# A written order for the output projection and the passage to up, scaling a step behind the store, and transposes in 64-row pairs, in a hybrid decoder block

## The chip, the cores and the metric

The kernel runs on one core of one Trainium2 chip. The metric is device time in microseconds (us) of one execution. The kernel before takes 2476.66 us, the median of three runs (2476.07 to 2476.84).

## The reference

One decoder layer on x (2048 rows of 1024, float32):

```python
mod = c_act @ w_ada[l] + b_ada[l]
sh1, sc1, gt1, sh2, sc2, gt2 = [m[:, None, :] for m in jnp.split(mod, 6, axis=-1)]
h = rms_norm(x, g_mix[l]) * (1.0 + sc1) + sh1
y = hybrid_mixer(h, w_in[l], ...)          # ends in y @ w_out
x = x + gt1 * y
h = rms_norm(x, g_ffn[l]) * (1.0 + sc2) + sh2
x = x + gt2 * conv_ffn(h, w_up[l], w_conv[l], b_conv[l], w_down[l])
```

The change concerns the stretch between the mixer and the feed-forward part: y @ w_out, the gated residual, the second RMSNorm with its scale and shift, and the turn of h into the layout (channels on partitions) that the up product reads.

## The kernel before, in words

All float32 products are made of three passes over values split in a high and a low part (`mm3`, L53): the matmuls on L54, L55 and L56, high times high, high times low, low times high. A split is a ScalarE copy into the high part and a VectorE subtraction into the low part.

The kernel has these stages in order of time: the first projection and the mLSTM and gating groups, the attention, the output projection (from about 1019 us), the passage to up, up with its convolution and gate, and down. From up on, products follow a scheme with seven products in place of eight, on sums and differences of quarters of h, called B11, B21, B22, T1, T2, T3 and T4.

The output projection works on four blocks of 512 rows, in the order `TBS = (2, 3, 0, 1)` (`n` is 0 to 3). A block is eight steps. A step is one row tile `i` (128 rows) times one half `nb` of the 1024 columns: 8 x 3 matmuls of 128x512 into one of four banks of PSUM (`Block.mm`, L1449, tiles wps). The order of (i, nb) is by halves in block 0 (all four tiles with nb = 0, then all with nb = 1), by tiles in blocks 1 and 2, and by pairs of tiles in block 3.

One step later the result is evicted on VectorE (`evict`, L1460). For nb = 0 it is multiplied with gt1 (L1465) and added to x (L1466); for nb = 1 the weights already hold gt1, and one addition does (L1468). ScalarE squares the half and sums it (L1469). After nb = 1 the row tile is stored to x2_d (L1471), `stats` (L1473) makes the RMS factor with two small VectorE operations and one power on GpSimd, and `scale` (L1479, L1481) multiplies the whole row tile with it, in place, so after its store has been read. Only the last two row tiles of block 3 are scaled into a fresh tile.

When the four row tiles of a block are scaled, `turns` (L1494) puts them through PE: per 128 columns `k`, `turn` (L1484) makes four 128x128 transposes into one bank (tile tps, four of them), and one ScalarE activation (L1490) applies scale and shift and writes the tile hz. Each block has two groups of four `turn`, put in behind its successor's second and third step. Block 3's eight `turn` stand in the passage, between up products.

For the second half of the rows (blocks 0 and 1) the parts of h are split and stored for later (`put`, L1421, `put_d`, L1436, to hc_d); `turns` puts them in the list `todo`, and `some` takes a few operations' worth of it at each step. The tiles that hold a split (tag w, four of them) later hold the first up weights (`w_load`, L344, called at step 3 of block 3).

Beside that, `load_w` (L314) loads the second half of w_out in eight parts, multiplies each with gt1 (L302) and splits it (L136, L137) into the sixteen tiles wo1; and `y_load` (L1317) and `y_split` (L1321) load, add and split the next block's eight y parts. Both use five load buffers (tag ld).

Each engine works through its own queue in order. SP issues all DMAs, also in order, and waits at an issue until the data or the buffer is free. Up to step 3 of block 3 a scheduler of the framework decides the order in which the recorded instructions stand on each engine. From step 4 of block 3 on they stand as the program writes them (`manual_schedule`, L1885), through the passage (L1923 to L2037) and until step 14 of up.

Of the kernel before, what the change touches and what calls it, by code (L numbers as in the profile page):

```python
# [8 lines left out]
F32 = mybir.dt.float32  # L9
F32R = mybir.dt.float32r  # L10
# [7 lines left out]
P = 128  # L18
# [15 lines left out]
def trunk(  # L34
# [254 lines left out]
    def load_parts(src, more=None):  # L289
        t = pool.tile([P, TB], F32, name="ld", tag="ld")  # L290
        dma(t, src)
        if more is None:
            return t, None
        t2 = pool.tile([P, TB], F32, name="ld", tag="ld")
        dma(t2, more)
        return t, t2

    def split_parts(t, t2, tag, eng, pair=False, gain=None):
        if t2 is not None:
            eng.tensor_tensor(t, t, t2, op=ALU.add)  # L300
        if gain is not None:
            eng.tensor_tensor(t, t, gain, op=ALU.mult)  # L302
# [11 lines left out]
    def load_w(nb, gain=None):  # L314
        for k in range(KT):
            src = w_out[k * P : (k + 1) * P, nb * 512 : nb * 512 + 512]
            eng = V if gain is not None else (G, V)[k % 2]
            wo.append(split_parts(*load_parts(src), "wo%d" % nb, eng, gain=gain))
# [1002 lines left out]
    def y_split(n=9):  # L1321
        while loaded_y and n:
            n -= 1
            n, k, parts = loaded_y.pop(0)
            ys.setdefault(n, {})[k] = split_parts(*parts, "act%d" % ((4 if n % 2 else 14) + k), V, pair=True)

    order = (
        "SUSSXSUVSUSSXSUXVSSSXVVYUSXSSTVXSUSVSXSSUWVXWUWXVXSSXUVYUWUXWVUWVWXUSSXSXSVVXVSXZSSSVVUSSUXWXVSSSXSV"
        "VVYUSSXSXVVVWUYSSXUVVVXSSWUWVXSSXSVUUWTVUXSSXSXSVVVZSXSXUWXVSSUYWVVXUUWVSSSXSVVXUSXSUVVWSSXSVXVSSZSV"
# [91 lines left out]
    def put(n, q, t):  # L1421

        if n == "T2":
            src = t[:, 1, :].bitcast(F32)
            V.tensor_tensor(src, h_part("B22", q), h_part("T1", q), op=ALU.subtract)
            V.tensor_tensor(h_part("T4", q), h_part("B21", q), src, op=ALU.subtract)
        else:
            src = h_part(n, q)
            if n == "T1":
# [3 lines left out]
        A.copy(t[:, 0, :], src)  # L1433
        V.tensor_tensor(t[:, 1, :], src, t[:, 0, :].bitcast(F32), op=ALU.subtract)

    def put_d(n, q):  # L1436
        t = pool.tile([P, 2, 512], F32R, name="hl", tag="w")
        put(n, q, t)
        dma(hc_d[COMBO.index(n), q], t.bitcast(F32))

    class Block:
        def __init__(self, n, tb):
# [3 lines left out]
        def rows(self, i):  # L1446
            return slice(self.tb * TB + i * P, self.tb * TB + i * P + P)

        def mm(self, i, nb):  # L1449
            if i not in self.x:  # L1450
                self.x[i] = pool.tile([P, D], F32, name="x2")
                dma(self.x[i], x[self.rows(i), :])
                self.st[i] = pool.tile([P, 2], F32, name="st", tag="wst_")
            sl = slice(i * P, (i + 1) * P)
# [26 lines left out]
            V.tensor_scalar(t, self.x[i], self.st[i][:, 0:1], None, op0=ALU.mult)  # L1481
            self.xn[i] = t

        def turn(self, k):  # L1484
            if self.half == 0:
                hT[k] = pool.tile([P, 1024], F32, name="hz", tag="zy")
            ps = pp.tile([P, 512], F32, name="tps", tag="tps")
            for i in range(4):
                T.transpose(ps[:, i * P : (i + 1) * P], self.xn[i][:, k * P : (k + 1) * P], ident)
            A.activation(  # L1490
                hT[k][:, self.half * 512 : self.half * 512 + 512], ps, AF.Identity, bias=sh2[:, k : k + 1], scale=a2[:, k : k + 1]
            )

        def turns(self, ks):  # L1494
            for k in ks:
                self.turn(k)
            names = ("T1", "T3", "T2", "T4", "B22") if self.half else ("B11", "B21")
            for group in (("T1",), ("B11",)) if ks[0] == 0 else (("T3",), ("T2", "T4", "B22"), ("B21",)):
                for q in range(4):
                    for n in group:  # L1500
                        if self.H == 1 and n in names:
                            ops = {"T1": 2, "T3": 2, "T2": 3}.get(n, 1)
                            todo.append((ops, lambda n=n, q=q: put_d(n, q)))

    hb = {}

# [18 lines left out]
            b_low(n, q)  # L1525

    def some(ops):
        while todo and ops > 0:
            n, f = todo.pop(0)
            ops -= n  # L1530
            f()

    def up_open_left():
        pool.open(
# [5 lines left out]
    class Group:  # L1540
# [37 lines left out]
        def prep(self, p):  # L1578
            self.sums(p)
            self.high(p)  # L1580
            self.low(p)
# [297 lines left out]
    prev = before = None  # L1879
    written = ExitStack()  # L1880
    for n, tb in enumerate(TBS):
        blk = Block(n, tb)
        for j, (i, nb) in enumerate((by_nb, by_i, by_i, by_two)[n]):
            if (n, j) == (3, 4):
                written.enter_context(tc.manual_schedule())  # L1885
            blk.mm(i, nb)
            if (n, j) == (0, 0):
                load_w(1, gt1[:, 512:1024])
            if (n, j) == (3, 3):
                w_first = [w_load(0), w_load(1)]  # L1890
            if prev:
                prev[0].evict(*prev[1:])
            y_split()
            if prev and prev[2] == 1:
                prev[0].stats(prev[1])
            some({1: 2, 2: 5, 3: 3}.get(n, 0))
            if (n, j) == (3, 7):
                prep(4)
            if prev and prev[2] == 1:
                prev[0].scale(prev[1], pool.tile([P, D], F32, name="x2") if (n, j) == (3, 7) else None)  # L1900
            if (n, j) == (3, 5):
                pool.close("wo_r")
                up_open_right()
                for _ in range(AHEAD):
                    up_groups(-1)
            if (n, j) == (3, 6):
                for m in range(4):
                    prep(m)
            if before and j in ((2, 3) if n == 3 else (1, 2)):
                assert n < 3 or not todo  # L1910
                before.turns(range(4) if j == (2 if n == 3 else 1) else range(4, 8))
            if n == 3 and j in (4, 5):
                b_first(("B11", "B21")[j - 4])
            if n < 3:
                for k in ({3: (0, 1), 4: (2, 3), 5: (4, 5), 6: (6, 7)}.get(j, ()) if n == 0 else {5: (5, 6), 6: (7,), 7: ()}.get(j, (j,))):
                    y_load(n + 1, k)
            prev = (blk, i, nb)
        before = blk
    assert not todo and not loaded_y
    blk.evict(3, 1)  # L1920
    blk.stats(3)
# [14 lines left out]
    at(7, "high")  # L1936
    blk.turn(0)
    b_diff("T1", 0)
    blk.turn(1)
    b_high("T1", 0)  # L1940
    b_diff("T1", 1)
    at(7, "low")
    for q in (2, 3):
        blk.turn(q)
        b_high("T1", q - 1)
        b_low("T1", q - 2)
        b_diff("T1", q)
# [1 line left out]
    blk.turn(4)  # L1949
    b_high("T1", 3)  # L1950
    b_low("T1", 2)
    blk.turn(5)
    b_low("T1", 3)
    b_diff("T2", 0)
    blk.turn(6)
    blk.turn(7)
    pp.close("wo_l")
    pp.open("up_l", "left", ("ub1", 2048, 4))
    pool.close("wo_l")
# [154 lines left out]
```

## Time and profile before

| | |
|---|---|
| median of three runs | 2476.66 us |
| the profiled execution, its time | 2478.34 us |
| the profiled execution, its span | 2476.6 us |
| PE busy | 2443.3 us, 99% |
| VectorE busy | 1876.7 us, 76% |
| ScalarE busy | 1198.8 us, 48% |
| granted PE clock, mean | 0.998 |
| output projection | 1019 to 1211 us of the span |
| passage to up | 1211 to 1250 us of the span |

The span is from the first to the last instruction of the profiled execution; the rest of its time lies around it. An engine's busy time counts its instructions' run times; PE's matmuls overlap each other, so that a busy PE is not a PE at its peak. A row of the time-line has start, length, engine, line, operation, tiles written and read, shape, and in brackets the idle time before it and who ended it. In the names, wps is a bank of the projection, tps one of the transposes, x a row tile, hz a turned tile, ub a bank of up.

### The profile page before, as it was taken

Reading aid. Unit: us, or ns where it says so; the run is one execution under the profiler, and the core shown is the slowest. Engines: PE = TensorE matmul, PEld = TensorE weight load, DVE = VectorE, ACT = ScalarE, POOL = GpSimd, SP = SyncE. Lnnn points to the kernel's source line nnn. Section 1 sums busy time; section 2 is a strip of 40 time slices with the busy share of each in tenths; the row PEclk is TensorE's granted clock in tenths of the full one; section 3 lists DMA queues with packets and bytes.
Section 4 is the critical chain, followed back from the end, with each engine's and each line's share of the span. In section 5 each row is a group of like instructions: output and inputs, shape, how many; then the busy total and the mean of one; then the engine's idle time right before and its main releaser. Section 6 shows DMA issues by size and latency. Waiting matters only on the chain.

```text
span 2476.6 us, 38891 instructions
## 1 busy us (share of the span) xinstructions
PE 2443.3 (99%) x14297; PEld 1984.7 (80%) x14297; DVE 1876.7 (76%) x3170; ACT 1198.8 (48%) x2068; POOL 379.7 (15%) x417
## 2 busy tenths in 40 slices
PE   6999999999999999999999999999999999999999
PEld 6888888888766666788878888888888888888887
DVE  6657656476377777756799888879888878988897
ACT  5443343433267778544554544445444445444443
POOL 2023310133257665200000000000000000000000
PEclk9999999999999999999999999999999999999999
DMA  8345753545665453677332222282222229387523
GB/s 271 105 148 164 219 170 91 152 139 162 160 171 152 118 164 107 209 252 285 100 103 86 85 85 77 85 314 94 77 85 85 86 95 319 126 285 238 174 73 119
DMA packets 297271, 373.48 MB, mean 151 GB/s; under 512 B 31358, under 2 KB 190044, under 8 KB 296056
## 3 DMA queue, kind: packets, MB, share of 16 engines
q1 hardware_dynamic: 297080, 371.00, 47.6%
q8 instruction: 112, 1.84, 0.3%
q14 instruction: 79, 0.65, 0.1%
HBM read 274.34 MB, written 96.58 MB: 150 GB/s over the span
## 4 chain that ended last, share of the span: by engine, by line
PE 86%; DVE 6%; DMA 5%; ACT 2%; issue 1%; POOL 0%; SPq 0%; DVEq 0%; ACTq 0%; POOLq 0%
PE ub L55 11%; PE ub L56 11%; PE ub L54 11%; PE acc L54 6%; PE acc L56 6%; PE acc L55 6%; PE db L55 5%; PE db L56 5%; PE db L54 5%; PE op L266 5%; PE pr L218 5%; PE pr L248 3%; DMA x_d<-x 1%; PE wps L56 1%; PE wps L54 1%
## 5 line engine op out<-in xcount | busy, mean ns | idle before, releaser
L54 PE MATMUL acc<-wh,hh 128*128 128x512 f32 (+2 forms) x752 | 279.2, 372 | 0.0
L54 PE MATMUL ub<-T,wsph 128*128 128x512 f32 x704 | 273.8, 389 | 1.2 <-ACT wsph L1572 1.2
L55 PE MATMUL ub<-T,wsph 128*128 128x512 f32 x704 | 274.3, 390 | 0.2 <-DVE T L1520 0.2
L56 PE MATMUL ub<-T,wspl 128*128 128x512 f32 x704 | 273.9, 389 | 0.0
L56 PE MATMUL acc<-wh,hl 128*128 128x512 f32 (+2 forms) x752 | 270.0, 361 | 0.3 <-DVE hl L586 0.2
L55 PE MATMUL acc<-wl,hh 128*128 128x512 f32 (+2 forms) x752 | 268.7, 359 | 0.6 <-DVE wl L628 0.6
L55 PE MATMUL db<-wspl,wsph 128*128 128x512 f32 x616 | 239.9, 390 | 0.1
L56 PE MATMUL db<-wsph,wspl 128*128 128x512 f32 x616 | 239.6, 389 | 0.0
L54 PE MATMUL db<-wsph 128*128 128x512 f32 x616 | 239.5, 389 | 0.0
L1572 ACT CAST wsph<-S 128x512 fp32r<-128x512 f32 x176 | 109.6, 624 | 219.0 <-PE ub L55 153.8
L1715 ACT CAST wsph<-act 128x512 fp32r<-128x512 f32 x154 | 96.3, 626 | 228.6 <-PE db L55 218.7
L55 PE MATMUL ub<-B,wsph 128*128 128x512 f32 x528 | 205.6, 389 | 1.0 <-DVE B L1520 0.9
L54 PE MATMUL ub<-B,wsph 128*128 128x512 f32 x528 | 205.7, 390 | 0.0
L56 PE MATMUL ub<-B,wspl 128*128 128x512 f32 x528 | 205.4, 389 | 0.0
L224 DVE CUSTOM_DVE_ANT_0 L<-pr,nf 128x1024 f32<-128x1024 f32 (+7 forms) x128 | 124.4, 989 | 67.7 <-PE pr L223 31.3
L232 ACT ACTIVATE L<-L,nm 128x1792 f32<-128x1792 f32 (+15 forms) x128 | 153.7, 1204 | 21.1 <-DVE nm L224 20.3
L56 PEld LDWEIGHTS acc<-wh,hl 128*128 128x128 f32 x752 | 142.3, 190 | 22.2 <-DVE hl L586 0.9
L55 PEld LDWEIGHTS acc<-wl,hh 128*128 128x128 f32 x752 | 142.8, 190 | 20.4 <-DVE wl L628 1.5
L54 PEld LDWEIGHTS acc<-wh,hh 128*128 128x128 f32 x752 | 142.8, 190 | 19.7 <-issue 0.7
L54 PEld LDWEIGHTS ub<-T,wsph 128*128 128x128 f32 x704 | 132.2, 188 | 29.2 <-ACT wsph L1572 1.6
L55 PEld LDWEIGHTS ub<-T,wsph 128*128 128x128 f32 x704 | 132.1, 188 | 28.7 <-DVE T L1520 1.5
L56 PEld LDWEIGHTS ub<-T,wspl 128*128 128x128 f32 x704 | 132.2, 188 | 27.5 <-DVE wspl L1576 0.3
(331 smaller groups left out, 5535.1 us busy)
## 6 DMA issues: line engine op xcount, KB each, us to landing
w<-in_w_up_dram SPq DMA_DIRECT2D x88, 512.0 KB
wd<-in_w_down_dram SPq DMA_DIRECT2D x154, 256.0 KB
wa<-in_w_ada_dram SPq DMA_DIRECT2D x96, 256.0 KB
act_d<-yc SPq DMA_DIRECT2D x44, 512.0 KB
act<-act_d SPq DMA_DIRECT2D x44, 512.0 KB
wr<-in_w_in_dram SPq DMA_DIRECT2D x64, 256.0 KB
q<-q_d SPq DMA_DIRECT2D x128, 128.0 KB
hc_d<-hl SPq DMA_DIRECT2D x28, 512.0 KB
```

What stands on the lines that cost most here:

```text
L54: T.matmul(ps, lh, rh, start=start, stop=False, skip_group_check=resume)
L55: T.matmul(ps, lh, rl, start=False, stop=False, skip_group_check=resume)
L56: T.matmul(ps, ll, rh, start=False, stop=stop, skip_group_check=resume)
L218: T.matmul(dst, q2[a][r, qs], kk[b][r, ks], start=n == 0, stop=n == 2 and not (last and f == own))
L224: V.tensor_tensor_reduce(out=L[:, c * 1024 : c * 1024 + w], in0=sp[:, o : o + w], in1=nf[:, c * 1024 + o : c * 1024 + o + w], scale=-1.0, ...
L232: A.activation(L, L, AF.Exp, bias=nm[:, n : n + 1], scale=-1.0, accum_out=rs)
L248: T.transpose(tp[:, f, to : to + 64], L_[h, tb, i][0][r, o : o + P], ident[r, r])
L266: T.matmul(op_[h, tb][r].rearrange("p (f n) -> p f n", f=2)[:, :, c0:], vv_[h // 2][:, 2 * p + j, h % 2 * 64 : h % 2 * 64 + 64], pT[:, :, ...
L1572: A.copy(self.wa[p][0], self.source(p))
L1715: A.copy(hi, v)
```

## The change

All of it lies between the end of the attention and the passage.

**Written order.** The whole output projection now stands as the program writes it. A step is, in this order: the low parts still held from the step before (`settle`); the matmuls; the scale of the row tile whose statistics were made a step before; the eviction of the step before; the splits of the step (`run`: y parts that have been loaded, in the first three steps of block 0 three parts of w1 each, and some of `todo`), where each task has a first VectorE operation, a ScalarE copy and a low part that is held until the next task's copy is issued; the loads of the next y parts; the load of the next x row tile (`want`); the statistics. Of `todo` four operations are taken per step in blocks 2 and 3 (before, five and three).

**Scaling.** `scale` follows one step behind `stats`, in place as before. In the last four steps of block 3 every row tile except the first is scaled into a fresh tile (before, the last two).

**Transposes.** `turn` takes two `k` at once. Each 128x128 transpose becomes two transposes of 64 rows, lower and upper half into two banks (tile tps, now two pairs of banks), as `turn_pair` (L238) does in the attention. The activation reads both banks.

```diff
+    def w1_task(k):
+        t = w1_parts[k]
...
+        return (
+            lambda: V.tensor_tensor(t, t, gt1[:, 512:1024], op=ALU.mult),
+            lambda: A.copy(hi, t),
+            lambda: V.tensor_tensor(lo, t, hi.bitcast(F32), op=ALU.subtract),
+        )
...
-    pp.open("wo_l", "left", ("tps", 2048, 4))
+    pp.open("wo_l", "left", ("tps", 4096, 2))
+    written = ExitStack()
+    written.enter_context(tc.manual_schedule())
+    for _ in range(5):
+        w1_load()
...
-        def turn(self, k):
...
-            for i in range(4):
-                T.transpose(ps[:, i * P : (i + 1) * P], self.xn[i][:, k * P : (k + 1) * P], ident)
...
+        def turn(self, k0):
+            ps = pp.tile([P, 2, 512], F32, name="tps", tag="tps")
+            for m in range(2):
+                k = k0 + m
...
+                for i in range(4):
+                    at = m * 256 + i * 64
+                    for f, r in enumerate((lower, upper)):
+                        T.transpose(ps[:, f, at : at + 64], self.xn[i][r, k * P : (k + 1) * P], ident[r, r])
+            for m in range(2):
+                k = k0 + m
+                to = hT[k][:, self.half * 512 : self.half * 512 + 512].rearrange("p (i f c) -> p f i c", f=2, c=64)
+                A.activation(
+                    to, ps[:, :, m * 256 : m * 256 + 256].rearrange("p f (i c) -> p f i c", c=64), AF.Identity,
+                    bias=sh2[:, k : k + 1], scale=a2[:, k : k + 1],
+                )
...
+    def run(tasks):
+        for first, high, low in tasks:
+            first()
+            high()
+            settle()
+            held.append(low)
+
+    def settle():
+        while held:
+            held.pop(0)()
...
+    for r, (n, j, i, nb) in enumerate(walk[:28]):
+        blk, before = blocks[n], blocks[n - 1] if n else None
+        settle()
+        blk.mm(i, nb)
+        if normed:
+            normed[0].scale(normed[1])
+            normed = None
+        tasks = [y_task() for _ in range(len(loaded_y))]
+        if prev:
+            prev[0].evict(*prev[1:])
+        if n == 0 and j < 3:
+            tasks += [w1_task(k) for k in range(3 * j, min(3 * j + 3, KT))]
+        tasks += some({1: 2, 2: 4, 3: 4}.get(n, 0))
+        run(tasks)
...
+        for k in y_wanted.get((n, j), ()):
+            y_load(n + 1, k)
+        n2, _, i2, _ = walk[r + 1]
+        if r < 27:
+            blocks[n2].want(i2)
+        if prev and prev[2] == 1:
+            prev[0].stats(prev[1])
+            normed = prev[:2]
...
+        if prev[2] == 1:
+            prev[0].scale(prev[1], pool.tile([P, D], F32, name="x2"))
```

How the rows move is shown at three places; outside the projection and the passage the order of PE, VectorE and ScalarE is the same in both programs, and VectorE's number of instructions too. First, PE at block 0's first group of transposes (x_13156 to x_13304 are its four row tiles, x_13168 to x_13309 in the change). Before:

```order
L54 MATMUL wps<-wo1h,yhl 128x512
L55 MATMUL wps<-wo1l,yhl 128x512
L56 MATMUL wps<-wo1h,yhl 128x512
L1489 MATMUL tps<-ident,x_13156 128x128
L1489 MATMUL tps<-ident,x_13240 128x128
L1489 MATMUL tps<-ident,x_13272 128x128
L1489 MATMUL tps<-ident,x_13304 128x128
```

After the change:

```order
L54 MATMUL wps<-wo1h,yhl 128x512
L55 MATMUL wps<-wo1l,yhl 128x512
L56 MATMUL wps<-wo1h,yhl 128x512
L1528 MATMUL tps<-ident,x_13168 128x64 x2
L1528 MATMUL tps<-ident,x_13216 128x64 x2
L1528 MATMUL tps<-ident,x_13263 128x64 x2
L1528 MATMUL tps<-ident,x_13309 128x64 x2
```

The group stands at the same place; it has 32 transposes of 64 rows (x2 is the pair of halves) for 16 of 128.

Second, VectorE at the end of block 0 (L1481 and L1516 are the scale, L1468 and L1503 the eviction of nb = 1, L300 and L1347 the sum of a y part, L137 and L1349 its low part). Before:

```order
L1475 TENSOR_TENSOR st<-st 128x1
L1476 TENSOR_SCALAR st<-st 128x1
L137 TENSOR_TENSOR yhl<-ld,yhl 128x512 x2
L1481 TENSOR_SCALAR x_13272<-x_13272,st 128x1024
L300 TENSOR_TENSOR ld<-ld 128x512
L1468 TENSOR_TENSOR x_13304<-wps,x_13304 128x512
L137 TENSOR_TENSOR yhl<-ld,yhl 128x512 x2
L1475 TENSOR_TENSOR st<-st 128x1
L1476 TENSOR_SCALAR st<-st 128x1
L137 TENSOR_TENSOR yhl<-ld,yhl 128x512 x3
L1481 TENSOR_SCALAR x_13304<-x_13304,st 128x1024
L1465 TENSOR_TENSOR yg<-wps,gt_13154 128x512
```

After the change:

```order
L1503 TENSOR_TENSOR x_13263<-wps,x_13263 128x512
L1510 TENSOR_TENSOR st<-st 128x1
L1511 TENSOR_SCALAR st<-st 128x1
L1349 TENSOR_TENSOR yhl<-ld,yhl 128x512
L1516 TENSOR_SCALAR x_13263<-x_13263,st 128x1024
L1503 TENSOR_TENSOR x_13309<-wps,x_13309 128x512
L1510 TENSOR_TENSOR st<-st 128x1
L1511 TENSOR_SCALAR st<-st 128x1
L1516 TENSOR_SCALAR x_13309<-x_13309,st 128x1024
L1500 TENSOR_TENSOR yg<-wps,gt_13166 128x512
```

The scale of row tile i stands ahead of the eviction of row tile i+1 in both; fewer y operations lie between.

Third, VectorE in block 3, around the scale of its second row tile (B is the split of a part of h). Before:

```order
L1468 TENSOR_TENSOR x_14364<-wps,x_14364 128x512
L1475 TENSOR_TENSOR st<-st 128x1
L1476 TENSOR_SCALAR st<-st 128x1
L1481 TENSOR_SCALAR x_14364<-x_14364,st 128x1024
L1468 TENSOR_TENSOR x_14408<-wps,x_14408 128x512
L1475 TENSOR_TENSOR st<-st 128x1
L1476 TENSOR_SCALAR st<-st 128x1
L1481 TENSOR_SCALAR x_14408<-x_14408,st 128x1024
L1520 TENSOR_TENSOR B_14604<-hz,B_14604 128x512
```

After the change:

```order
L1503 TENSOR_TENSOR x_14392<-wps,x_14392 128x512
L1510 TENSOR_TENSOR st<-st 128x1
L1511 TENSOR_SCALAR st<-st 128x1
L1516 TENSOR_SCALAR x_14392<-x_14392,st 128x1024
L1503 TENSOR_TENSOR x_14438<-wps,x_14438 128x512
L1510 TENSOR_TENSOR st<-st 128x1
L1511 TENSOR_SCALAR st<-st 128x1
L1516 TENSOR_SCALAR x_14687<-x_14438,st 128x1024
L1563 TENSOR_TENSOR B_14689<-hz,B_14689 128x512
```

The second row tile's scale now writes another tile (x_14687) than the one that is being stored (x_14438).

More of the change, by code (lines that the diff above doesn't have):

```diff
@@ L312, in trunk, with w1_load @@
     wo = []
[L314 to L318, printed above, removed]
+    w1_parts = []
+    def w1_load():
+        k = len(w1_parts)
+        if k < KT:
+            w1_parts.append(load_parts(w_out[k * P : (k + 1) * P, 512:1024])[0])
+    def w1_task(k):
+        t = w1_parts[k]
+        wo.append((pool.tile([P, TB], F32R, name="wo1h", tag="wo1"), pool.tile([P, TB], F32R, name="wo1l", tag="wo1")))
+        hi, lo = wo[8 + k]
+        return (
[3 more added lines that the diff above has]
+        )
     def up_open_right():
@@ L1432, in put, with low @@
                 V.tensor_tensor(src, h_part("B22", q), h_part("B12", q), op=ALU.subtract)
[L1433 to L1439, printed above, removed]
+        def low():
+            V.tensor_tensor(t[0][:, 1, :], source(), t[0][:, 0, :].bitcast(F32), op=ALU.subtract)
+            dma(hc_d[COMBO.index(n), q], t[0].bitcast(F32))
+        return first, lambda: A.copy(t[0][:, 0, :], source()), low
     class Block:
@@ L1527, in some @@
     def some(ops):
+        tasks = []
         while todo and ops > 0:
-            n, f = todo.pop(0)
+            n, q = todo.pop(0)
             ops -= n
-            f()
+            tasks.append(put_task(*q))
+        return tasks
+    held = []
+    def run(tasks):
[7 more added lines that the diff above has]
+            held.pop(0)()
     def up_open_left():
@@ L1878, in trunk @@
     by_two = [(i + m, nb) for m in (0, 2) for nb in range(2) for i in range(2)]
[L1879 to L1918, printed above, removed]
@@ new lines, in trunk @@
+    for j, (i, nb) in enumerate(by_two):
+        if j < 4:
+            continue
+        blk.mm(i, nb)
+        if normed:
+            normed[0].scale(normed[1])
+            normed = None
+        prev[0].evict(*prev[1:])
+        if prev[2] == 1:
+            prev[0].stats(prev[1])
+        if j == 7:
+            prep(4)
+        if prev[2] == 1:
+            prev[0].scale(prev[1], pool.tile([P, D], F32, name="x2"))
+        if j == 5:
+            pool.close("wo_r")
+            up_open_right()
+            for _ in range(AHEAD):
+                up_groups(-1)
+        if j == 6:
+            for m in range(4):
+                prep(m)
+        if j in (4, 5):
+            b_first(("B11", "B21")[j - 4])
+        prev = (blk, i, nb)
```

69 lines of the change are left out of this document (48 added, 21 removed).

## The prediction, on record before the change was run

> **What bounds the kernel now.** I read the page's first part, then the stretches around the change, then TensorE's (PE's) time-line there, then the chain of waits. In the page's first part and in a table of stretches, the columns are busy microseconds by engine (PE, weight loads, VectorE, ScalarE, GpSimd), granted clock, DMA share, GB/s.
>
> ```profile
> span 2476.6 us, 38891 instructions
> PE 2443.3 (99%) x14297; PEld 1984.7 (80%) x14297; DVE 1876.7 (76%) x3170; ACT 1198.8 (48%) x2068; POOL 379.7 (15%) x417
> ...
> 1019.00:1211.00 192.00, 190.68 (x890) 158.77 (x889) 117.71 (x210) 82.27 (x165) 10.34 (x16) 1.00 0.70 238
> 1211.00:1250.00 39.00, 37.33 (x176) 29.58 (x175) 37.14 (x61) 24.71 (x46) 0.17 (x1) 1.00 0.36 108
> 1250.00:1312.00 62.00, 62.00 (x274) 51.13 (x273) 61.33 (x81) 36.18 (x62) 0.00 (x0) 1.00 0.29 94
> ```
>
> PE is the bound, at full clock. The output projection runs from 1019 to 1211, and PE lacks only 1.3 us of 192 there; VectorE has 74 us to spare. In the passage to up (1211 to 1250) both are nearly full: VectorE 37.1 of 39, PE 37.3. So the projection gets shorter only by shorter PE work or by the 1.3 us, and the passage only by what VectorE lets through. Behind 1250 VectorE is as full as PE, so what arrives there as a shift stays a shift.
>
> Where PE's time goes besides the matmuls is in the eight groups of transposes. The rows: start, length, engine, line, tiles, count, idle before and its cause.
>
> ```profile
> 1073.60 0.49 PE L1489 MATMUL tps<-ident,x 128*128 128x128 f32 x3
> 1074.84 1.64 PE L1489 MATMUL tps<-ident,x 128*128 128x128 f32 x13 [0.75 <-DVE x L1481]
> 1076.23 0.48 PE L54 MATMUL wps<-wo0h,yhl 128*128 128x512 f32 x1
> 1076.55 0.39 PE L55 MATMUL wps<-wo0l,yhl 128*128 128x512 f32 x1
> 1076.78 0.40 PE L56 MATMUL wps<-wo0h,yhl 128*128 128x512 f32 x1
> ...
> 1081.81 1.91 PE L1489 MATMUL tps<-ident,x 128*128 128x128 f32 x16
> 1083.47 0.48 PE L54 MATMUL wps<-wo1h,yhl 128*128 128x512 f32 x1
> ...
> 1121.69 0.49 PE L1489 MATMUL tps<-ident,x 128*128 128x128 f32 x3
> 1122.75 1.64 PE L1489 MATMUL tps<-ident,x 128*128 128x128 f32 x13 [0.57 <-DVE x L1481]
> 1124.15 0.48 PE L54 MATMUL wps<-wo0h,yhl 128*128 128x512 f32 x1
> ```
>
> From the first transpose to the next matmul, an undisturbed group of 16 lasts 1083.47 - 1081.81 = 1.66 us, 104 ns each. The first group lasts 2.63 and the third 2.46: at the fourth transpose PE waits for the last scaled row tile (L1481). The second, fourth, fifth and sixth are undisturbed. Matmuls follow each other in 0.23 us (1076.55 to 1076.78), the first behind a group in 0.32. Six groups lie in the projection and cost 2.63 + 2.46 + 4 x 1.66 = 11.73 us; two lie in the passage.
>
> **Part 1, the transposes.** Each 128-row transpose becomes two of 64 rows. The kernel has this form already, in the attention (L248), same shapes, halves alternating:
>
> ```profile
> 1008.63 1.27 PE L248 MATMUL pr<-ident,L 64*128 64x64 f32 x34
> 1009.83 3.02 PE L266 MATMUL op<-pT,vv 128*64 128x512 f32 x16
> ...
> 1012.78 1.40 PE L248 MATMUL pr<-ident,L 64*128 64x64 f32 x38
> 1014.10 1.30 PE L266 MATMUL op<-pT,vv 128*64 128x512 f32 x8
> ```
>
> 34 take 1.20 us until the next matmul, 38 take 1.32: 30 ns for one more, and some 0.18 us fixed, with a change of array shape at each end. A group of 32 then takes 1.20 - 2 x 0.03 = 1.14 us instead of 1.66. Bounds: 0.96 (no fixed part) and 1.32 (the row of 38). Undisturbed, six groups cost 6.84 us: 11.73 - 6.84 = 4.89 us less, if the two waits go (Part 2). The bounds move this by +1.1 and -1.1. ScalarE still reads each group with four instructions of 512 columns; with 82 of 192 us busy it hides them behind the next step's 5.6 us of PE (1076.23 to 1081.81). If it did not, the second group of a block would wait for its bank pair.
>
> The Trainium skill, page "TensorEngine Tiling (Array Packing)", section "Key Properties", speaks against the change: switching the tiling mode drains the array, and here every group brings two switches that the 128-row form lacks. The fixed 0.18 us above contains two switches; by the rule alone a 128 x 128 neighbour could cost more, which is the third rival.
>
> **Part 2, scaling a step behind the store.** The row tile is stored unscaled and then scaled in place, so each scale waits for its store. VectorE in block 0, and the stores in the chain of waits:
>
> ```profile
> 1048.87 0.68 DVE L1468 TENSOR_TENSOR x<-wps,x 128x512 f32<-128x512 f32 x1
> 1054.65 0.75 DVE L1481 TENSOR_SCALAR x<-x,st 128x1024 f32<-128x1024 f32 x1
> 1055.32 0.68 DVE L1468 TENSOR_TENSOR x<-wps,x 128x512 f32<-128x512 f32 x1
> ...
> 1069.22 0.69 DVE L1468 TENSOR_TENSOR x<-wps,x 128x512 f32<-128x512 f32 x1
> 1074.03 0.75 DVE L1481 TENSOR_SCALAR x<-x,st 128x1024 f32<-128x1024 f32 x1 [0.18 <-DMA x_d<-x]
> ...
> 1049.69 4.86 DMA x_d<-x
> 1056.03 5.34 DMA x_d<-x
> 1062.84 5.01 DMA x_d<-x
> ...
> 1098.40 3.71 DMA x_d<-x
> 1118.23 3.62 DMA x_d<-x
> ```
>
> Eviction to store takes 0.82 (1048.87 to 1049.69), scale to next eviction 0.67. The scale of row i stands ahead of the eviction of row i+1, now and in the change (second piece of order above), so in block 0, which takes its second halves in a run, the four stores stay in series: last scale = first eviction + 4 x (0.82 + store) + 3 x 0.67 = first eviction + 5.3 + 4 stores. With 4.8 us a store this gives 1073.4; the trace has 1074.03.
>
> In the change, what differs is the start and the store. The start: from gt1's arrival VectorE has the same 30-odd operations in both.
>
> ```profile
> 1028.54 1.90 DVE L302 TENSOR_TENSOR ld<-ld,gt 128x512 f32<-128x512 f32 x3 [8.72 <-DMA gt<-gt_d]
> 1042.91 3.87 DMA ld<-y_d
> ```
>
> SP still issues the same five weight loads and then gt1, so VectorE still begins at 1028.5. In the written order each step's eviction stands first and low parts wait for their own ScalarE copy; the third y part needs the fifth-last load buffer and so stands behind one load (3.87). I put the first eviction 1.7 us later, 1050.6 (bounds 1048.9 and 1051.4). The store: now y loads are issued whenever one of five buffers falls free, beside the stores; in the change each y part is asked for one step ahead and its low half is held, so that fewer are under way. I take 4.0 us, near the lone stores (3.62 and 3.71; upper bound 5.34). The last scale ends at 1050.6 + 5.3 + 16 + 0.75 = 1072.7; PE wants it where its idle time began, at 1074.84 - 0.75 = 1074.1. Up to a store of 4.3 us the wait is gone, and the next thing late is nothing on VectorE but PE itself. The third group's wait goes with more room: blocks 1 and 2 evict second halves every other step, and the scale stands a step of 5.6 us behind.
>
> Costed at nothing, with their cover, are the rest. The w1 parts (w_out times gt1) must be split when PE reads them:
>
> ```profile
> L54 PE MATMUL wps<-wo1h,yhl x128: 387/389/482, 1041.0 to 1205.1; 128*128 128x512 f32 x128
> ```
>
> The first read is at 1041.0, that of the eighth part 7 x 3 x 0.23 = 4.8 us later, at 1045.8. VectorE has 16 operations of 0.63 (three in 1.90) and three evictions of two such before the last part: 14 us, to 1042.5, so 3.3 us of cover; each us beyond is a us of PE. What stands behind a waiting scale on VectorE is the next eviction; PE waits for that only when all four banks are full, three steps on. The y parts of the next block are due a step after their last split. The held low halves delay the hc_d stores, behind which SP issues the first four up weights, needed three steps (some 16 us) later. GpSimd keeps its 16 small powers. VectorE and ScalarE have the same number of instructions.
>
> **Part 3, the passage.** The second row tile of block 3 is now scaled into a fresh tile (third piece of order above); its scale waited 2.75 us for its store.
>
> ```profile
> 1189.41 0.75 DVE L1481 TENSOR_SCALAR x<-x,st 128x1024 f32<-128x1024 f32 x1 [2.75 <-DMA x_d<-x]
> ...
> 1205.54 0.39 PE L56 MATMUL wps<-wo1h,yhl 128*128 128x512 f32 x1
> 1207.46 0.68 DVE L1468 TENSOR_TENSOR x<-wps,x 128x512 f32<-128x512 f32 x1
> 1211.21 1.91 PE L1489 MATMUL tps<-ident,x 128*128 128x128 f32 x16
> ...
> 1212.54 0.58 ACT L1606 COPY s<-ub 128x512 f32<-128x512 f32 x1
> 1213.54 1.45 ACT L1490 ACTIVATE hz<-tps,sh,a 128x512 f32<-128x512 f32 x2
> ...
> 1246.67 0.49 PE L55 MATMUL ub<-B,wsph 128*128 128x512 f32 x1 [0.85 <-DVE B L1520]
> ```
>
> The 2.75 us wait made VectorE late until 1211: the last eviction began at 1207.46, though PE was done at 1205.93. Without it, eviction, scale and weight sums come 1.5 us sooner; ScalarE's copy of the second up product cannot start before 1211.2, so its first reading of the transposes comes 1212.54 - 1211.3 = about 1.1 us sooner (the following copies take the same time). From there VectorE is full and PE ends up waiting for it (1246.67). So here PE's own shorter groups are worth nothing, and VectorE's earlier start is the gain: 1.1 us (0 if it is not earlier, 1.7 if PE's shorter groups count in full).
>
> **The sum.** 4.89 + 1.1 = 6.0 us. The profiled execution took 2478.34 us, 1.7 over its span and 1.7 over the median of 2476.66; I take the 6.0 off both: 2472.3 and 2470.7. 0.2%, about what a measurement of this kernel can tell from no change, is 4.95 us, so the forecast lies 1 us beyond it.
>
> **The rivals.** First: block 0's stores stay at 4.8 us. Then the last scale ends at 1050.6 + 5.3 + 19.2 + 0.75 = 1075.9, PE waits 1.8 (2.0 with a restart like that in the 2.63), the gain is 4.0 and the time 2472.7. For it: most stores of that stretch took 5. Against: fewer loads in flight. Chance 0.2.
>
> Second, slower: the halves do not run side by side here. If each took the 104 ns of a present transpose, a group takes 3.33, six groups 20.0 instead of 11.73: 8.2 lost, less the 1.1, so 2483.8. It decides from 67 ns a half block (6 x 32 x 67 ns = 11.73 + 1.1). Against: 30 ns in the attention. Chance 0.07.
>
> Third: the shape changes next to 128 x 128 matmuls cost more than next to the attention's. The first matmul behind a group takes 0.09 more than its next already. With 0.15 us more for each of 12 changes the gain is 6.0 - 1.8 = 4.2 and the time 2472.5. By the skill's rule the sum would be this one. Chance 0.13.
>
> Fourth: the change does not do what it says in block 0 or in the passage, since the scale still stands ahead of the next eviction and the passage's start is set by something else: only 4 x 0.52 + 0.8 + 0.5 = 3.4, time 2473.3. Chance 0.06.
>
> **How the numbers follow.** The forecast has 0.54; nine tenths of it, and a little of the first and third, are beyond 0.2%: faster 0.53. The rest of these and the fourth are within: same 0.37. Slower takes the second and 0.03 for a wait that I don't see: 0.10. Range: the gain from 1.8 (first rival, with the dear transposes and nothing in the passage: 4.0 - 1.1 - 1.1) to 7.1 (the cheap transposes): 2469.6 to 2474.9.
>
> **What would show it.** Right: groups of 32 half transposes lasting 1.1 to 1.2 us; no idle before them in blocks 0 and 1; the first reading of the transposes in the passage a us nearer to the last projection matmul. Wrong: a wait for L1516's x inside the first group; 64-row transposes spaced by more than 40 ns; PE waiting for wo1 parts near 1041; ScalarE holding the second group of a block.

## The result, and the profile after

The changed kernel takes 2503.66 us (median of five runs, 2499.15 to 2505.65) against 2476.07 for the kernel before, run beside it (five runs, 2475.03 to 2476.84): a ratio of 1.0109, 95% interval 1.0097 to 1.0120. It is 27.6 us slower where 6.0 us faster was forecast. The profiled execution took 2503.66 us with a span of 2501.9: 25.3 us more than the 2478.34 of before.

The first part of the changed kernel's page, and its stretches around the change with the prediction's bounds (they answer to the rows 1019 to 1211, 1211 to 1250 and 1250 to 1312 there):

```profile
PE 2449.7 (98%) x14425; PEld 1984.9 (79%) x14425; DVE 1877.3 (75%) x3170; ACT 1197.2 (48%) x2068; POOL 381.6 (15%) x417
```

```profile
1019.00:1211.00 192.00, 173.66 (x887) 139.21 (x884) 101.81 (x179) 71.72 (x142) 10.30 (x13) 0.95 0.68 219
1211.00:1250.00 39.00, 36.52 (x205) 29.49 (x204) 28.58 (x51) 22.55 (x43) 2.11 (x4) 0.96 0.44 142
1250.00:1312.00 62.00, 60.94 (x266) 49.05 (x265) 60.58 (x88) 34.19 (x63) 0.00 (x0) 1.00 0.30 92
```

In the first stretch PE now lacks 18.3 us of 192 where it lacked 1.3, and its granted clock has fallen from 1.00 to 0.95. VectorE is less busy there than before (101.8 against 117.7), and so are the DMA engines (0.68 against 0.70): nothing in that stretch works harder, so something waits. PE's waits between 1019 and 1260 (us in total, times, longest), by whom it waits for:

```profile
PE wps L54 <- ACT yhl L1344: 15.7, 5, 6.2
PE tps L1528 <- ACT hz L1532: 3.7, 4, 1.6
PE tps L1528 <- DVE x L1516: 1.0, 1, 1.0
PE wps L56 <- DVE yhl L1349: 0.5, 1, 0.5
```

yhl are the split y parts, which the prediction had costed at nothing. PE's time-line shows where: one group of transposes, then the entries to blocks 2 and 3, then block 2's second group of transposes (it stands among block 3's steps) and the passage.

```profile
1080.90 0.39 PE L56 MATMUL wps<-wo0h,yhl 128*128 128x512 f32 x1
1081.22 1.21 PE L1528 MATMUL tps<-ident,x 64*128 64x64 f32 x32
1082.36 0.50 PE L54 MATMUL wps<-wo1h,yhl 128*128 128x512 f32 x1
1082.70 0.39 PE L55 MATMUL wps<-wo1l,yhl 128*128 128x512 f32 x1
...
1114.13 0.50 PE L54 MATMUL wps<-wo0h,yhl 128*128 128x512 f32 x1 [0.86 <-ACT yhl L1344]
...
1122.41 0.80 PE L54 MATMUL wps<-wo0h,yhl 128*128 128x512 f32 x1 [6.18 <-ACT yhl L1344]
1123.00 0.63 PE L55 MATMUL wps<-wo0l,yhl 128*128 128x512 f32 x1
1123.43 0.63 PE L56 MATMUL wps<-wo0h,yhl 128*128 128x512 f32 x1
...
1173.12 0.50 PE L54 MATMUL wps<-wo0h,yhl 128*128 128x512 f32 x1 [3.04 <-ACT yhl L1344]
...
1181.95 0.79 PE L54 MATMUL wps<-wo0h,yhl 128*128 128x512 f32 x1 [5.38 <-ACT yhl L1344]
...
1203.90 0.71 PE L1528 MATMUL tps<-ident,x 64*128 64x64 f32 x16 [1.55 <-ACT hz L1532]
1205.24 0.71 PE L1528 MATMUL tps<-ident,x 64*128 64x64 f32 x16 [0.63 <-ACT hz L1532]
...
1242.49 0.71 PE L1528 MATMUL tps<-ident,x 64*128 64x64 f32 x16 [1.34 <-ACT hz L1532]
```

The group lasts 1082.36 - 1081.22 = 1.14 us, as forecast. But the matmuls behind the long waits follow each other in 0.43 us (1123.00 to 1123.43) instead of 0.23: PE restarts at half its clock (granted 0.50 there, shown in the last section).

A measure that the rest leans on: for each kernel, the start of the matmul behind each group of transposes, counted from the first projection matmul in its own time-line, minus the same in the kernel before. Negative is a lead, positive a lag, in us. The last column is a matmul of the up products (at 1287.6 in the kernel before); to the end it changes by less than 1 us. It is one profiled execution of each kernel. The rows below the first are the experiments'.

| kernel | block 0: 1st, 2nd | block 1 | block 2 | passage | in up |
|---|---|---|---|---|---|
| changed | -1.4, -1.8 | 7.5, 7.1 | 19.2, 21.3 | 23.7, 24.4 | 25.5 |
| changed, hc_d stores late | -1.4, -1.8 | -3.0, -3.5 | -3.9, -4.3 | -0.6, -0.5 | -0.1 |
| changed, y loads early | -1.4, -1.8 | -3.0, -3.5 | -3.9, -0.6 | 2.3, 3.0 | 3.5 |
| changed, 128-row transposes | -1.0, -1.0 | 5.2, 5.2 | 16.7, 18.3 | 21.2, 21.6 | 21.2 |
| before, 64-row transposes | -1.4, 1.9 | 3.0, 2.5 | 2.1, 1.7 | 1.4, 0.8 | 1.2 |
| stores late, third row's x first | -1.4, -1.8 | -3.0, -3.5 | -3.9, -4.3 | -4.7, -5.2 | -4.7 |
| stores late, both rows' x first | -1.4, -1.8 | -3.0, -3.5 | -3.9, -3.8 | -4.2, -5.0 | -4.5 |
| both rows' x first, 128-row transposes | -1.0, -1.0 | -1.8, -1.9 | -1.9, -1.9 | -1.9, -2.6 | -3.0 |
| both rows' x first, scale not a step behind | -1.4, -1.8 | -3.0, -3.5 | -3.9, -3.4 | -3.7, -3.0 | -2.5 |

(The group of a block stands behind the second or third step of its successor, so the loss at the entry to block 2 shows in the column of block 1.) The changed kernel leads by 1.8 us through block 1, loses 10.5 at the entry to block 2 (to a lag of 8.7 just ahead of the next group) and 12.5 at the entry to block 3 (7.1 to 19.6), 2.1 at block 2's second group with 1.6 of slow clock behind it, and 2.6 in the passage (22.9 to 25.5).

**Why the y parts come late.** SP's queue in block 1 of the changed kernel; yt_d and y_d are the two addends of one y part (the last four of a block's eight parts have only the first), hc_d the stored parts of h:

```profile
1089.65 0.43 SPq L291 DMA_DIRECT2D ld<-yt_d  x1
1090.12 0.78 SPq L295 DMA_DIRECT2D ld<-y_d  x1
...
1100.26 0.32 SPq L1469 DMA_DIRECT2D hc_d<-hl  x1
1100.63 0.42 SPq L291 DMA_DIRECT2D ld<-yt_d  x1
1101.15 6.58 SPq L1469 DMA_DIRECT2D hc_d<-hl  x2
1107.79 1.25 SPq L291 DMA_DIRECT2D ld<-yt_d  x2
```

VectorE and ScalarE there:

```profile
1097.56 0.69 DVE L1347 TENSOR_TENSOR ld<-ld 128x512 f32<-128x512 f32 x1 [7.10 <-DMA ld<-y_d]
1098.94 0.69 DVE L1349 TENSOR_TENSOR yhl<-ld,yhl 128x512 fp32r<-128x512 f32 x1 [0.69 <-ACT yhl L1344]
1099.55 0.69 DVE L1468 TENSOR_TENSOR hl<-hz,hl 128x512 fp32r<-128x512 f32 x1
```

```profile
1098.29 0.62 ACT L1344 CAST yhl<-ld 128x512 fp32r<-128x512 f32 x1 [7.01 <-DVE ld L1347]
```

Read as a loop: the y load issued at 1090.12 lets VectorE add at 1097.56; ScalarE casts at 1098.29; the low part follows at 1098.94; only behind it, at 1099.55, stands the held low part of an h split; its hc_d store leaves SP at 1100.26; and only behind that store stands the next y load, 1100.63. That is 11.0 us from one part's load to the next (1089.65 to 1100.63), and 7.2 for the one after, against a step of 5.6. Of the 11.0, 7.4 pass between the issue of the load and its sum (1090.12 to 1097.56). In the kernel before the loads run ahead of it all. SP's queue there: the last four of block 2's loads, then the fifth part of block 3 and its last three:

```profile
1064.14 5.52 SPq L291 DMA_DIRECT2D ld<-yt_d  x4
...
1085.79 0.32 SPq L291 DMA_DIRECT2D ld<-yt_d  x1
...
1112.90 1.77 SPq L291 DMA_DIRECT2D ld<-yt_d  x3
```

All of block 2's loads have left by 1070, and five parts of block 3 by 1086, before an hc_d store stands in the queue: the scheduler had bunched the loads, the written order spreads them, mostly one part a step, behind the stores.

### The profile page after: what moved, and what is told of

It reads as the page before. It is cut to its first block, busy times and chain, and to the rows that moved or that the text cites. A ratio compares the mean times of both kernels' runs of the same rounds, so it can differ in the third digit from the quotient of the medians.

```text
span 2501.9 us, 39146 instructions
## 1 busy us (share of the span) xinstructions
PE 2449.7 (98%) x14425; PEld 1984.9 (79%) x14425; DVE 1877.3 (75%) x3170; ACT 1197.2 (48%) x2068; POOL 381.6 (15%) x417
## 4 chain that ended last, share of the span: by engine, by line
PE 50%; DVE 1%; ACT 1%; DMA 0%; issue 0%; POOL 0%; ACTq 0%; DVEq 0%
PE ub L54 11%; PE ub L56 11%; PE ub L55 11%; PE db L55 6%; PE db L54 6%; PE db L56 6%; DMA x<-in_x_dram 0%; ACT hz L1532 0%; DVE wspl L1635 0%; DVE hz L1554 0%; DVE B L1563 0%; DVE T L1563 0%; ACT yg L1504 0%; ACT wsph L1631 0%; DVE x L1501 0%
## 5 line engine op out<-in xcount | busy, mean ns | idle before, releaser
L232 ACT ACTIVATE L<-L,nm 128x1792 f32<-128x1792 f32 (+15 forms) x128 | 153.6, 1203 | 21.2 <-DVE nm L224 18.8
L54 PEld LDWEIGHTS acc<-wh,hh 128*128 128x128 f32 x752 | 142.9, 190 | 19.6 <-issue 0.7
```

Source lines behind the costliest of these rows:

```text
L54: T.matmul(ps, lh, rh, start=start, stop=False, skip_group_check=resume)
L232: A.activation(L, L, AF.Exp, bias=nm[:, n : n + 1], scale=-1.0, accum_out=rs)
```

## Experiments

The theory: the loop through SP's queue. The rivals: the loads are slow because they share the DMA with the stores; or the 64-row transposes themselves cost the time. The first four ran with 27 runs of the kernel before (median 2476.57), the last four with 33 (2476.73).

**Transposes alone.** The kernel before with `turn`, `turns` and the tps pool of the change.

```diff
-    pp.open("wo_l", "left", ("tps", 2048, 4))
+    pp.open("wo_l", "left", ("tps", 4096, 2))
...
-            for k in ks:
+            for k in ks[::2]:
                 self.turn(k)
```

> The kernel before with the 64-row transposes alone; the order of the other work is left to the scheduler, as before. If the halves are what Part 1 of the prediction says (1.14 us a group instead of 1.66), PE gains 0.52 us in each of six groups, 3.1 us, and the two waits for the scaled row tile (0.75 and 0.57 us) stay: 2476.1 - 3.1 = 2473.0 us. If the slower time comes from the halves themselves, this kernel is slower than the kernel before by several us.

Measured: 2477.76 us, ratio 1.0001 (0.9992 to 1.0010). Neither: no gain, no several us of loss. The table shows 1.4 gained at the first group, 1.2 at the third and 0.4 at each later one, but 3.3 lost at the second, and 2.3 of slow clock behind it (1.9 to 4.2, before the third group's gain). ScalarE, then PE, at that place:

```profile
1079.99 0.63 ACT L1469 ACTIVATE yg<-x 128x512 f32<-128x512 f32 x1 [3.35 <-DVE x L1468]
...
1080.62 2.77 ACT L1497 ACTIVATE hz<-tps,sh,a 128x512 f32<-128x512 f32 x4
```

```profile
1082.10 0.78 PE L1493 MATMUL tps<-ident,x 64*128 64x64 f32 x16 [2.37 <-ACT hz L1497]
```

ScalarE holds the first group's reading behind a square that waits for an eviction, and the second group's banks aren't free. PE's saving brought it to a neighbour that was not ready; why VectorE's eviction stood late there (it waits for a y load) was read from the trace, not tried.

The expectation missed in the waits too: it had the two for the scaled row tile stay, and neither is there. VectorE's last scale of block 0, then PE at the first group:

```profile
1071.10 0.76 DVE L1481 TENSOR_SCALAR x<-x,st 128x1024 f32<-128x1024 f32 x1
```

```profile
1072.84 1.21 PE L1493 MATMUL tps<-ident,x 64*128 64x64 f32 x32
```

Up to that scale VectorE and SP have the same operations in the same order as in the kernel before. Yet it begins 52.9 us behind the first projection matmul (at 1018.19 here), and 55.0 behind it in the kernel before (1074.03 - 1019.04). The difference is in the times alone, from where VectorE first has gt1 on: 8.3 against 9.5 us behind that matmul. At the third group PE came 4 us later than before, and the row tile was ready. One execution of each does not tell how often the kernel before has the first wait.

**y loads early.** The changed kernel with the loads of blocks 1 and 2 asked for ahead of the step's eviction and tasks.

```diff
         tasks = [y_task() for _ in range(len(loaded_y))]
+        if n:
+            for k in y_wanted.get((n, j), ()):
+                y_load(n + 1, k)
...
-        for k in y_wanted.get((n, j), ()):
-            y_load(n + 1, k)
+        if n == 0:
+            for k in y_wanted.get((n, j), ()):
+                y_load(n + 1, k)
```

> The changed kernel with one thing moved: in blocks 1 and 2 the y part's loads are asked for ahead of the step's eviction and tasks, so ahead of that step's x_d and hc_d stores in SP's queue, and two parts can be under way instead of one. Theory (a loop through SP's queue: load, add, cast, lows, hc_d store, next load, 9 to 11 us a part against a step of 5.4): the waits for the y parts at the start of blocks 2 and 3 (16.2 us of idle PE, and the slow clock behind them) go, and the time falls by 17 to 23 us, to 2481 to 2487. Rival (traffic: the loads take 5 to 7 us because the stores share the DMA engines, whatever the order): the loads still arrive one in 9 us or so and the time stays above 2497.

Measured: 2479.69 us, ratio 1.0009 (1.0000 to 1.0018). The theory holds: PE waits for no y part any more, and 24.0 us are gone, a little more than its 17 to 23. It leads by 3.9 us into block 3, and then loses 3.3 at block 2's second group, 1.4 in slow clock behind it and 2.7 in the passage. The first of these on PE:

```profile
1178.96 0.71 PE L1528 MATMUL tps<-ident,x 64*128 64x64 f32 x16 [2.58 <-ACT hz L1532]
```

VectorE ten us ahead of it, in the kernel with early y loads (its x_d store stands behind an hc_d store in SP's queue) and, in the second fence, in the next one (where it stands ahead):

```profile
1167.75 0.75 DVE L1516 TENSOR_SCALAR x<-x,st 128x1024 f32<-128x1024 f32 x1 [2.10 <-DMA x_d<-x]
```

```profile
1163.62 0.75 DVE L1516 TENSOR_SCALAR x<-x,st 128x1024 f32<-128x1024 f32 x1 [0.89 <-DMA x_d<-x]
```

**hc_d stores late.** The changed kernel; a step's hc_d stores are issued behind its y loads. The step's x load still stands behind them, since `store()` stands ahead of `want`; the expectation puts the stores behind it too, which this edit does not do.

```diff
-            dma(hc_d[COMBO.index(n), q], t[0].bitcast(F32))
+            stores.append((hc_d[COMBO.index(n), q], t[0].bitcast(F32)))
...
         for k in y_wanted.get((n, j), ()):
             y_load(n + 1, k)
+        store()
```

> The changed kernel with the hc_d stores alone moved: each is issued at the end of its step, behind the y loads and the x load, VectorE's and ScalarE's order unchanged. Theory (the loop through SP's queue): the y loads no longer stand behind a store that waits for the last load's work, the waits at blocks 2 and 3 go as in the kernel with earlier y loads, 2481 to 2487. If it is not the stores in front but that the load is asked for in the step before it is needed, it stays above 2495.

Measured: 2476.96 us, ratio 0.9999 (0.9989 to 1.0008). Only SP's order differs from the changed kernel, and 26.7 us are gone, more than the theory's 17 to 23: block 2's second group waits no more either; the x_d store too stands ahead of the hc_d stores now. Block 2's fifth part (1100.63 in the changed kernel) and the sixth and seventh (1107.79) in its SP queue:

```profile
1086.19 0.47 SPq L291 DMA_DIRECT2D ld<-yt_d  x1
...
1088.85 2.40 SPq L291 DMA_DIRECT2D ld<-yt_d  x2
```

This kernel's projection begins 3.1 us sooner in its span (1016.7 against 1019.8), so the fifth part leaves 11.4 us earlier than in the changed kernel and the sixth 15.9.

The rival of shared traffic alone falls: the same bytes move, and the wait is gone. That the traffic lengthens each load, and with it the loop, is not excluded. In all six groups of this kernel there is no wait, and the lead grows to 4.3 us; the passage then eats it whole.

**128-row transposes back in the changed kernel.** `turn`, `turns` and the pool as before the change, the rest as changed.

> The changed kernel with the 128-row transposes put back, everything else in its written order. If the late y parts set PE's time in blocks 2 and 3, the shorter transposes of blocks 2 and 3 were worth little there and the time is 2503.7 plus 1 to 3. If the halves cost something in the written order (for ScalarE, which waits in the second group of block 3 for 2.2 us), it is faster than 2503.7.

Measured: 2498.01 us, ratio 1.0080 (1.0066 to 1.0094). So in the changed kernel the halves gain nothing: they cost 4.3 us by the table, 5.7 by the medians. The table says where: the loss at the entries to blocks 2 and 3 is smaller (-1.0 to 6.0, and to 16.7 at the entry to block 3 against 19.6), and so is the one at block 2's second group (16.7 to 18.3, against 19.2 to 21.3 with 1.6 of slow clock behind it). That group waits for ScalarE with the slower transposes too, but the clock stays at 1.00:

```profile
1198.91 2.66 PE L1524 MATMUL tps<-ident,x 128*128 128x128 f32 x16 [0.71 <-ACT hz L1525]
```

It lasts 2.41 us to the next matmul (at 1201.32) in place of 1.66. Why the loop turned some tenths of a us faster each time with the longer groups I did not settle. A part of a change has no price of its own while something else is late.

**Third row's x first.** On top of the late stores, for what the passage lost. The kernel with late stores there: VectorE, then SP at the last of the four up weights (the first was issued at 1176.0), then PE:

```profile
1190.65 0.69 DVE L1501 TENSOR_TENSOR x<-x,yg 128x512 f32<-128x512 f32 x1 [5.42 <-DMA x<-in_x_dram]
```

```profile
1181.48 1.79 SPq L359 DMA_DIRECT2D w<-in_w_up_dram  x1
1183.32 1.72 SPq L1484 DMA_DIRECT2D x<-in_x_dram  x1
```

```profile
1208.35 1.65 PE L1528 MATMUL tps<-ident,x 64*128 64x64 f32 x26 [3.03 <-DVE x L1516]
```

The up weights go into the tiles that the hc_d stores still hold, so they keep SP until 1183.3, and the x load stands behind them, which VectorE wants for block 3's third row at 1185.2 (1190.65 - 5.42).

```diff
             settle()
             store()
-            w_first = [w_load(0), w_load(1)]
         if before and j in ((2, 3) if n == 3 else (1, 2)):
...
             before.turns(range(4) if j == (2 if n == 3 else 1) else range(4, 8))
+        if (n, j) == (3, 3):
+            blk.want(2)
+            w_first = [w_load(0), w_load(1)]
```

> The kernel with late hc_d stores, and besides the x load of block 3's third row tile issued ahead of the four up-weight loads instead of behind them. In the kernel with late hc_d stores PE is 4.3 us ahead of the kernel before after the sixth group of transposes, and has lost all of it when the up products begin; VectorE waits 5.4 us there for this x load (issued 1183.3, landed 1190.5). Theory (the up weights stand in front of it in SP's queue, and VectorE carries its wait to the passage): the wait goes, PE keeps the 4.3 us, 2472.3, or up to 1.1 more by the prediction's third part, 2471.2. Rival (VectorE's own work bounds the passage, whatever x does): within 0.5 us of the kernel with late hc_d stores, 2477.

Measured: 2473.53 us, ratio 0.9988 (0.9979 to 0.9997); by the table the lead in up is 4.7 us, in the profiled runs. The theory holds, the rival falls: the passage follows x. Against the kernel with late stores 4.6 us are gone by the table and 3.4 by the medians.

**Both rows' x first.** One line more, `blk.want(3)` behind `blk.want(2)`.

> As the one before, and the fourth row tile's x load ahead of the up weights too. If 4 to 5 us from issue to landing make the fourth row late once the third is on time (it is issued at 1185.6 and would be read near 1190), this is up to 1 us faster than the one before, 2471; otherwise the same.

Measured: 2471.59 us, ratio 0.9981 (0.9972 to 0.9989), the fastest: 5.1 us below the kernel before. Against the one before the intervals overlap, and the table gives 4.5 against 4.7: the same. Its PE lacks 0.2 us of 192 between 1019 and 1211 (busy 191.78).

**Both rows' x first, with 128-row transposes.** 

> As the one before, with 128-row transposes. Prices Part 1 where nothing else is late: six groups of 0.52 us and the two in the passage, so 3.1 to 4.2 us slower than with the halves, 2474.5 to 2475.5. If the passage is bound by VectorE, whatever PE saves is lost there, and it is the same within 1 us.

Measured: 2474.55 us, ratio 0.9993 (0.9983 to 1.0002), 3.0 us slower than with the halves by the medians and 1.5 by the table. With nothing else late the halves gain 0.4 a group, 2.4 by the sixth (-1.9 here against the -4.3 of the kernel with only the third row's x first); the passage takes some of that.

**Both rows' x first, with the scale in the step of its store.**

```diff
             prev[0].stats(prev[1])
-            normed = prev[:2]
+            prev[0].scale(prev[1])
```

> As the kernel with both x loads first, but each row tile is scaled in the step of its store, as before the change, not a step behind it (Part 2 undone). VectorE then waits about 4 us for each store with its tasks behind it; the prediction's two waits (0.75 and 0.57 us) come back, so 1 to 2 us slower, 2472 to 2474; if VectorE's waits reach the y parts or ScalarE's reading of the transposes, 5 us and more.

Measured: 2475.20 us, ratio 0.9991 (0.9981 to 1.0000), 3.6 us slower by the medians, 2.0 by the table, between the two cases that were expected. And the expectation missed where: the waits at the first and third group do not come back (-1.4 and -3.0 as with the scale behind). The loss lies at block 2's second group (0.5) and in the passage (1.5).

## Why the prediction was wrong, point by point

**The step that failed** is a term put at nothing, in Part 2, "Costed at nothing, with their cover": "The y parts of the next block are due a step after their last split", and "The held low halves delay the hc_d stores, behind which SP issues the first four up weights, needed three steps (some 16 us) later". The up weights were followed past the delayed stores; the y loads, which the written order puts behind the same stores, were not. So the wait for the y parts was put at nothing, and it is 16.2 us of idle PE at the entries to blocks 2 and 3. Moving the stores alone brings 26.7 us back, of the 27.6 by which the change is slower. The same part even used the fact on the wrong side: "each y part is asked for one step ahead and its low half is held, so that fewer are under way" was counted as shorter stores, when one part under way means that a part takes the whole loop, 7 to 11 us, in a step of 5.6.

**None of the rivals named this.** The slower one (halves that do not run side by side) is refuted by the group of 1.14 us; the 0.03 for an unseen wait was all that stood for a wait of 16 us.

**Part 1** was right: 1.14 us a group, measured 1.14 in five of the six groups. What it missed is the entry. In the kernel before, from the last matmul to the first transpose:

```profile
1081.58 0.39 PE L56 MATMUL wps<-wo0h,yhl 128*128 128x512 f32 x1
1081.81 1.91 PE L1489 MATMUL tps<-ident,x 128*128 128x128 f32 x16
```

0.23 us; in the change 0.32 (1080.90 to 1081.22), and 0.34 behind the group in place of 0.32. So the change of shape costs 0.11 us a group, and six groups 0.66: 4.89 - 0.66 = 4.2, and the measured lead without other waits is 4.3. That is the third rival's mechanism at a third of its price. By the Trainium skill, page "TensorEngine Tiling (Array Packing)", section "Key Properties", switching the tiling mode drains the array; the trace fits that, at 0.09 us going in and 0.02 coming out, but can't tell a drain from another cost of the new shape.

**Part 2**, the stores of block 0: the two waits are gone, but the reason given is not borne out. VectorE's first eviction and last scale of block 0 in the changed kernel:

```profile
1050.65 0.68 DVE L1503 TENSOR_TENSOR x<-wps,x 128x512 f32<-128x512 f32 x1
...
1069.95 0.75 DVE L1516 TENSOR_SCALAR x<-x,st 128x1024 f32<-128x1024 f32 x1 [1.83 <-DMA x_d<-x]
```

The first eviction was forecast at 1050.6, the last scale's end at 1072.7; it is 1070.7. But the waits stay gone with the scale in its old place, and they are gone in the kernel before with 64-row transposes alone, in VectorE's old order up to block 0's last scale. So the step behind is not needed for it, and what took the waits away is not shown. 1.8 us of the 4.89 (2.63 + 2.46 - 2 x 1.66) stood on them.

**Part 3**: not right in the changed kernel. In place of 1.1 us gained the passage loses 2.6. The one wait was taken off the second row; the first row's scale, still in place, now has a longer one:

```profile
1209.95 0.75 DVE L1516 TENSOR_SCALAR x<-x,st 128x1024 f32<-128x1024 f32 x1 [3.77 <-DMA x_d<-x]
```

In the kernel with late stores the passage loses 4.2 to a transfer that nobody waits for in the kernel before, the third row's x load. That is the question the prediction should have asked of its own 4.9 us: who is next late if PE comes 4 us sooner. With that load moved, the passage gains 0.4 to 0.7 us, inside the forecast's 0 to 1.7.

**What the waits cost** is more than their length. At the entries to blocks 2 and 3, at block 2's second group and in the passage the slow clock behind them cost 1.5 to 2.5 us each, by the lag's growth until the matmuls are at 0.23 us again; of the 25.5 us that is 7.

The kernel with both x loads first, 2471.59, comes within 1 us of the forecast's 2470.7, but only with two moves in SP's order that the change did not make.

## What to carry to other kernels

When an order is written by hand, follow every queue, above all the one that issues transfers: for each load list what stands ahead of it and what that waits for, and see whether the wait leads back to the load before; a loop like that sets a pace of its own, whatever the engines' shares say. Keep loads ahead of stores that wait for compute, and give a step's loads to the queue before its work. A faster engine is worth only the slack of its neighbours: after each gain, ask for the transfer or the reader that was just on time.

## What the runs showed of the hardware that was not expected

PE's clock drops behind a wait, and late. The changed kernel at the entry to block 2, PE without work from 1116.2 to 1122.4 (columns as in the stretches above, the clock third from the end):

```profile
1116.00:1120.00 4.00, 0.23 (x1) 0.00 (x0) 1.04 (x2) 0.00 (x0) 0.09 (x1) 1.00 0.70 284
1120.00:1121.00 1.00, 0.00 (x0) 0.00 (x0) 0.96 (x2) 0.00 (x0) 0.00 (x0) 0.89 0.01 4
1122.40:1127.00 4.60, 4.59 (x11) 3.58 (x12) 1.87 (x5) 0.72 (x2) 0.55 (x1) 0.50 0.53 142
```

The granted clock falls to 0.50 some 4.5 us after the idle time begins and stays there through 1127: matmuls at 0.43 in place of 0.23 us, 2.5 us by the lag on top of the 6.2 of the wait.

How long a wait must be is not one number here. Waits of 1.55 and 0.63 us with 16 transposes between them were enough (the rows at 1203.90 and 1205.24, 1.6 us more by the lag); a wait of 0.86 (1114.13) was not. In the passage of the changed kernel a wait of 1.34 us (1242.49), with one of 0.16 two us earlier (1240.43), was enough. The clock fell less than 3 us after it began, and the mean of the next microsecond is 0.50:

```profile
1243.00:1244.00 1.00, 1.00 (x11) 0.83 (x6) 1.00 (x2) 1.00 (x2) 0.17 (x1) 0.83 0.00 0
```

In the kernel with early y loads the same two waits, behind one of 1.71, left the clock at 1.00:

```profile
1212.02 1.02 PE L1528 MATMUL tps<-ident,x 64*128 64x64 f32 x26 [1.71 <-DVE x L1516]
...
1218.21 0.71 PE L1528 MATMUL tps<-ident,x 64*128 64x64 f32 x16 [1.34 <-ACT hz L1532]
```

The Trainium skill, page "TensorE: Matmul & The Clock Gate", section "What's actually happening", has the half clock after an idle window of about 3.4 us that runs free of the kernel; the trace agrees on the half, and equal waits with unequal outcomes fit a window that runs free, but 2.2 us of idle within 3 us already brought the half clock.
